# PEER block: u rows gathered for 64 more tokens, and all dense u ahead of all dense v

## Chip, cores and metric

The kernel runs on one core of a Trainium2 chip. The metric is the device time of one execution in microseconds (us). Engines are named as in the profile: PE is TensorE (PEld its weight loads), DVE VectorE, ACT ScalarE, POOL GpSimd, SP the queue that issues most transfers.

## What is computed

One decoder layer over 512 tokens of width 2048: a mixer (attention and mLSTM heads, not touched here), its output projection, and PEER, a layer with 16384 single-neuron experts. Each token takes 16 experts for each of 8 heads; cut to what matters:

```python
q = (xt @ w_q).reshape(T, PEER_HEADS, 2, PEER_KEY_DIM // 2)
scores = jnp.einsum('thpd,pnd->thpn', q, keys)
s_top, i_top = lax.top_k(scores, PEER_TOPK)
cand = ...            # 16 x 16 sums of the two halves
s_fin, pos = lax.top_k(cand, PEER_TOPK)
gate = jax.nn.softmax(s_fin, axis=-1)
ub = jnp.take(u, ib, axis=0)
act = jax.nn.gelu(jnp.einsum('thkd,td->thk', ub, xb), approximate=False) * gb
vb = jnp.take(v, ib, axis=0)
y = jnp.einsum('thk,thkd->td', act, vb)
```

## The kernel before, in words

The 512 tokens are four token tiles of 128. Token tile 0 is done sparsely: for each of its 128 (head, choice) slots POOL gathers one row of u for each token (128 rows of 8 KB in one indirect transfer, L588), DVE forms the dot with the normalised activations (L603); later the same with v (L614). The other three tiles, ND = 384 tokens, are done densely: TensorE multiplies all 128 blocks of 128 experts (u products into `sacc`, 48 matmuls a block, 384 columns each), and the chosen experts' gates stand in a table over all experts, zero elsewhere. The table is made with one-hot vectors: for each token two one-hots of 128 columns (`o`, one of them weighted with the gates, L887 and L893) are multiplied on TensorE (`gp_`), copied into `stg` by ACT (L896) and stored to memory (`gtab`). u products times gates, split into two parts, are `wbuf`; v products (`y`, 512 columns each) have them as weights. A group is 8 blocks; NEARLY = 68 blocks' u products are made early, beside the expert choice and the gate tables (`early_steps`, stored in `stab`), the other 60 between the v products of the groups that need them (`gated`, L938).

Every matrix is multiplied in two parts: `stream_split` (L101) loads 512 KB into one of three `raw` buffers, ACT casts the upper part `hi` (L109), DVE subtracts the lower part `lo` (L111), and TensorE takes hi and lo in three products. A new `raw` can be loaded when both have read the old one.

The order on each engine is made by a scheduler at build time from the order of the program and its priorities; a lower part gets its place 35 instructions earlier. Each engine then runs strictly in that order. The gathers are paced: `advance(n)` issues n of them at a place in the program, and each waits for the ACT cast before it (L590). Three `row` buffers hold the rows, two of them ahead of the one in use. SP issues all other transfers in one order, and one that waits holds up those behind it.

Stages in the profiled execution: mixer up to 636 us; output projection, with token tile 0's queries and choice, to about 921; choice for tiles 1 to 3 to 1374; gate tables to 1660; then u and v to the end.

Of the kernel before, what the change touches and what calls it, by code (L numbers as in the profile page):

```python
# [81 lines left out]
def block_kernel(ctx: ExitStack, tc: tile.TileContext, a, out):  # L82
# [35 lines left out]
    def project_nat(psA, src, parts, hook=None):  # L118
        """[tokens, 512 columns] of part.T @ w, one bank for each token tile."""
# [16 lines left out]
    def project_t(psA, src, xT):  # L136
        """[256 columns, tokens] of w.T @ xT, one bank for each 128 columns."""
# [27 lines left out]
    def transpose_split(psB, src, dst, groups=range(4)):  # L165
        """src [128 tokens, 2048] -> dst [128, hi/lo, kc, tokens]."""
# [28 lines left out]
    with ExitStack() as mx:  # L195
# [43 lines left out]
        # gates in rows: 0..7 fox forget, 32..35 mlstm input, 64..67 mlstm forget  # L239
# [5 lines left out]
        def gate_rows():  # L245
            # x2 is free until the mixer's first heads: 16 slots of 512 columns
# [24 lines left out]
            # log1p(ex) = ln(u) + (ex - (u - 1)) / u  # L271
# [11 lines left out]
            # fox: F = cumsum(log_sigmoid), in two parts in rows 0.. and 32.. of cF, with ones in  # L283
            # rows 64.. and 96..; bF has ones against the parts and -F against the ones
# [11 lines left out]
            # mlstm: b = within-chunk cumsum, e = i - b  # L296
# [13 lines left out]
            # running maximum M of e (from the state's), m = b + M  # L310
# [25 lines left out]
        def gate_cols(rowx, ones4, mprev, Mr):  # L336
            # columns: 0.. exp(-m), 32.. exp(m_prev - M), 64.. exp(e - M_last), 96.. exp(m_prev - M_last)
# [175 lines left out]
        def head_norms(t, lo, n, width):  # L513
            """heads of `width` columns from column lo, in place."""
# [24 lines left out]
        # from here on the transposed mixer output, then the transposed x3  # L539
        xtx.close()  # L540
        xdp = ctx.enter_context(tc.tile_pool(name="xdp", bufs=1, side="right"))
# [14 lines left out]
    stab = gdram.tile([NEARLY, P, ND], F32, name="stab")  # L556
    gtab = gdram.tile([NTG, P, NI * TG], F32, name="gtab")

    def tpool(stack, name, bufs=1):
        return stack.enter_context(tc.tile_pool(name=name, bufs=bufs, reuse_waits="tile"))  # L560
# [3 lines left out]
    idx0 = pc.tile([P, SLOTS], I32, name="idx0")  # L564
    gate0 = pc.tile([P, SLOTS], F32, name="gate0")
    dots = pc.tile([P, SLOTS], F32, name="dots")
    act0 = pc.tile([P, SLOTS], F32, name="act0")
    rows = tpool(ctx, "rows", 3)

    def dense_steps(ps, tag, i0, dst):  # L570
        """dst = gelu(u x3) of expert block i0, [experts, dense tokens], in 8 steps."""
        acc = ps.tile([P, 512], F32, tag=tag, name="sacc")[:, 0:ND]
        for s in range(2):
            hi, lo = stream_split(a["uT"][i0, s])
# [8 lines left out]
        nc.scalar.activation(out=dst, in_=acc, func=AF.Gelu)  # L583
        yield

    def gather(src, j):
        row = rows.tile([P, D], F32, tag="row", name="row")
        ins = nc.gpsimd.indirect_dma_start(  # L588
            out=row, out_offset=None, in_=a[src],
# [4 lines left out]
        return row  # L594

    def sparse_steps():
        ahead = []
        for j in range(SLOTS + LAG):
            if j < SLOTS:
                ahead.append(gather("u", j))  # L600
# [53 lines left out]
    with ExitStack() as rx:  # L654
# [190 lines left out]
        for _ in first:  # L845
            pass
# [220 lines left out]
```

## Time and profile before

| | us |
|---|---|
| median of 3 runs | 3297.2 (3293.05 to 3298.24) |
| profiled execution, its own time | 3298.24 |
| its span, first to last instruction | 3298.2 |
| PE busy | 3245.6 (98%) |
| DVE busy | 2293.9 (70%) |
| ACT busy | 1242.8 (38%) |
| POOL busy | 473.8 (14%) |

The durations of matmuls in the profile overlap, as they are pipelined; the time that one costs is the distance from its start to the next one's. The chain of work that ended last is followed back from the last instruction, at each step to what released it. A group's "idle before" is the idle time of its engine just ahead of its instructions. The granted clock was 0.996 of full speed over the span.

### The profile page before, as it was taken

The numbers are of one execution on the slowest core, as the hardware profiler recorded it, in microseconds if no ns is written. First come the engines' busy times: TensorE is split into PE (matmuls) and PEld (weight loads), VectorE is DVE, ScalarE is ACT, GpSimd is POOL, SyncE is SP. The second block draws the span as 40 slices with busy tenths as digits, with TensorE's granted clock in tenths as the row PEclk, the third lists the DMA queues.
The fourth block names the chain that finished last, engine by engine and source line by source line (L and its number), as shares of the span: only waits on it lengthen the run. The fifth ranks groups of instructions, "written<-read, shape, count | busy, mean of one in ns | idle before, by whom it ended". The sixth has DMA issues, their size and how long they took to land.

```text
span 3298.2 us, 43394 instructions
## 1 busy us (share of the span) xinstructions
PE 3245.6 (98%) x16681; PEld 2886.8 (88%) x16681; DVE 2293.9 (70%) x3746; ACT 1242.8 (38%) x1667; POOL 473.8 (14%) x380
## 2 busy tenths in 40 slices
PE   8999999999999999999999999999999999999998
PEld 6788787778799999999998888888899899898997
DVE  5542324467888989988867778876777767677774
ACT  4432223355554444455533333333233233232333
POOL 0000000100112323200012211111211112122110
PEclk9999999999999999999999999999999999999999
DMA  4232232266657667676788888887787887777774
GB/s 149 77 90 83 77 96 71 84 228 198 218 166 250 232 244 259 231 252 223 252 319 301 309 302 300 314 307 273 277 287 272 295 283 272 281 279 273 283 269 140
DMA packets 194065, 751.69 MB, mean 228 GB/s; under 512 B 19265, under 2 KB 61505, under 8 KB 158145
## 3 DMA queue, kind: packets, MB, share of 16 engines
q1 hardware_dynamic: 156994, 480.47, 41.8%
q0 software_dynamic: 36864, 268.45, 22.8%
q8 instruction: 131, 2.15, 0.3%
q14 instruction: 76, 0.62, 0.1%
HBM read 706.12 MB, written 42.73 MB: 227 GB/s over the span
## 4 chain that ended last, share of the span: by engine, by line
PE 73%; DMA 8%; issue 8%; DVE 7%; POOL 2%; ACT 1%; POOLq 0%; DVEq 0%; SPq 0%; ACTq 0%
PE y L116 24%; PE acc L116 22%; PE sacc L116 21%; DMA row<-in_u,idx 3%; DMA row<-in_v,idx 2%; DVE lo L111 2%; POOL row L588 2%; DMA raw<-in_w_out 1%; DVE x L614 1%; DMA stab<-es 1%; DMA raw<-in_uT 1%; PE sps L116 1%; ACT hi L109 1%; PE po L116 1%; DVE row L603 1%
## 5 line engine op out<-in xcount | busy, mean ns | idle before, releaser
L109 ACT CAST hi<-raw 128x1024 fp32r<-128x1024 f32 x736 | 773.8, 1052 | 1525.7 <-PE y L116 505.3
L111 DVE TENSOR_TENSOR lo<-raw,hi 128x1024 fp32r<-128x1024 f32 x736 | 900.6, 1227 | 514.4 <-ACT hi L109 513.3
L116 PE MATMUL sacc<-x3d,hi 128*128 128x384 f32 x4096 | 1052.7, 337 | 0.4 <-ACT x3d L173 0.4
L116 PE MATMUL y<-hi,wbuf 128*128 128x512 f32 x3048 | 942.0, 390 | 0.0
L116 PEld LDWEIGHTS sacc<-x3d,hi 128*128 128x128 f32 x4096 | 735.1, 188 | 1.2 <-ACT x3d L173 0.6
L116 PE MATMUL sacc<-x3d,lo 128*128 128x384 f32 x2048 | 686.0, 335 | 1.9 <-DVE lo L111 1.9
L116 PEld LDWEIGHTS y<-hi,wbuf 128*128 128x128 f32 x3048 | 572.9, 188 | 118.8
L116 PE MATMUL y<-lo,wbuf 128*128 128x512 f32 x1524 | 594.4, 390 | 5.2 <-DVE lo L111 5.0
L614 DVE SCALAR_TENSOR_TENSOR x<-row,act,x 128x2048 f32<-128x2048 f32 x128 | 300.9, 2351 | 138.3 <-DMA row<-in_v,idx 137.2
L116 PEld LDWEIGHTS sacc<-x3d,lo 128*128 128x128 f32 x2048 | 385.0, 188 | 4.4 <-DVE lo L111 4.4
L603 DVE SCALAR_TENSOR_TENSOR row<-row,x 128x2048 f32<-128x2048 f32 x128 | 293.8, 2295 | 120.3 <-DMA row<-in_u,idx 120.2
L116 PEld LDWEIGHTS y<-lo,wbuf 128*128 128x128 f32 x1524 | 286.4, 188 | 67.1 <-DVE lo L111 7.9
L588 POOL DMA_INDIRECT row<-in_u,idx x128 | 196.4, 1534 | 822.7 <-ACT hi L109 377.8
L588 POOL DMA_INDIRECT row<-in_v,idx x128 | 182.4, 1425 | 778.3 <-ACT hi L109 673.5
L116 PE MATMUL acc<-xT,hi 128*128 128x512 f32 x768 | 243.8, 395 | 0.0
L116 PE MATMUL acc<-hi,xT 128*128 128x512 f32 x768 | 241.8, 393 | 0.0
L116 PEld LDWEIGHTS acc<-hi,xT 128*128 128x128 f32 x768 | 143.8, 188 | 28.5
L116 PEld LDWEIGHTS acc<-xT,hi 128*128 128x128 f32 x768 | 143.7, 189 | 28.4 <-ACT xT L173 0.3
L116 PE MATMUL acc<-lo,xT 128*128 128x512 f32 x384 | 151.1, 393 | 0.0
L116 PE MATMUL acc<-xT,lo 128*128 128x512 f32 x384 | 150.4, 392 | 0.0
L156 POOL TENSOR_TENSOR rsr<-rst,mhalf 128x1 f32<-128x1 f32 (+2 forms) x24 | 19.0, 795 | 838.5 <-DVE rst L153 735.6
L893 DVE TENSOR_SCALAR o<-cst,i0T,gT 128x128 f32<-128x128 f32 x384 | 113.8, 345 | 35.5 <-PE gp__12799 L116 1.3
(522 smaller groups left out, 3073.6 us busy)
## 6 DMA issues: line engine op xcount, KB each, us to landing
raw<-in_uT SPq DMA_DIRECT2D x256, 512.0 KB, 5.0
raw<-in_vS SPq DMA_DIRECT2D x256, 512.0 KB, 5.1
raw<-in_w_out SPq DMA_DIRECT2D x64, 512.0 KB, 4.3
raw<-in_w_q SPq DMA_DIRECT2D x64, 512.0 KB, 4.5
gtab<-stg SPq DMA_DIRECT2D x12, 2048.0 KB, 7.5
gt<-gtab SPq DMA_DIRECT2D x16, 1536.0 KB, 9.8
raw<-in_w_fqk SPq DMA_DIRECT2D x32, 512.0 KB, 3.6
stab<-es SPq DMA_DIRECT2D x68, 192.0 KB, 4.4
```

What stands on the lines that cost most here:

```text
L109: pace[0] = nc.scalar.copy(out=hi[:, :width], in_=raw[:, :width]).ins
L111: nc.vector.tensor_tensor(out=lo[:, :width], in0=raw[:, :width], in1=hi[:, :width].bitcast(F32), op=OP.subtract)
L116: nc.tensor.matmul(out=o, lhsT=l, rhs=r, start=start, stop=stop)
L156: nc.gpsimd.tensor_tensor(out=r, in0=t, in1=mhalf[:, 0:width], op=OP.pow)
L588: ins = nc.gpsimd.indirect_dma_start(out=row, out_offset=None, in_=a[src], in_offset=bass.IndirectOffsetOnAxis(ap=idx0[:, j:j + 1], axis=0))
L603: nc.vector.scalar_tensor_tensor(out=row, in0=row, scalar=1.0, in1=x30, op0=OP.mult, op1=OP.mult, accum_out=dots[:, j - LAG:j - LAG + 1])
L614: nc.vector.scalar_tensor_tensor(out=x2[:, 0, :], in0=row, scalar=act0[:, j - LAG:j - LAG + 1], in1=x2[:, 0, :], op0=OP.mult, op1=OP.add)
L893: nc.vector.tensor_scalar(out=o0, in0=iota, scalar1=i0T[:, t:t + 1], scalar2=gT[:, t:t + 1], op0=OP.is_equal, op1=OP.mult)
```

## The change

1. Of token tile 1, the first NS = 64 tokens leave the dense u products, whose matmuls have DU = 320 columns in place of 384. Their u rows are gathered: 64 tokens x 128 slots are laid over 128 partitions as two halves of 64 slots, so 64 more gathers and dots. Their activations come back through a transpose (`act1`) into the gate table as weights, so v stays dense for all 384 tokens.
2. All 128 blocks of u products now come ahead of all v products. 118 of them are made beside the choice (2 + 56), ten gate tables (30) and alone (30); HOLD = 10 are kept for the last two tables, those of the 64 tokens, which need the gathered dots. Their results are stored to memory and read back two blocks at a time.
3. In the v stage the weights `wbuf` have two buffers, so that one group's are made beside the products of the group before; the first 512 columns' accumulators (`yk`) stay in PSUM over all groups. y has five banks in place of six.
4. In the gate tables one DVE comparison of 1024 columns makes the one-hots of both keys of four tokens (`on`), and ACT weights one of them (`og`).
5. The first four heads' queries of token tile 0 come ahead of the output projection of tiles 2 and 3; the gathers start there. The softmax of the gates is done once for each token tile.

```diff
-NEARLY = 68
-EARLY_TOPK = (1, 1, 2)
-EARLY_0 = 3
-EARLY_G = 2
-PACE_EARLY = 1.4
-PACE_G = 1.0
-PACE_V = 1.0
+NS = 64
+R = P // NS
+S1 = SLOTS // R
+DU = ND - NS
+FIRST_HEADS = 4
+EARLY_0 = 2
+EARLY_TOPK = (2, 2, 3)
+EARLY_G = 3
+HOLD = 10
+PACE_O = 0.4
+PACE_EARLY = 1.15
+PACE_G = 1.5
+PACE_U = 1.5
...
-                mm(acc, uh, x3d[:, 0, kc, :], kc == 0, False)
-                mm(acc, uh, x3d[:, 1, kc, :], False, False)
-                mm(acc, ul, x3d[:, 0, kc, :], False, kc == KC - 1)
+                mm(acc, uh, x3d[:, 0, kc, NS:], kc == 0, False)
+                mm(acc, uh, x3d[:, 1, kc, NS:], False, False)
+                mm(acc, ul, x3d[:, 0, kc, NS:], False, kc == KC - 1)
...
+        for r in range(R):
+            nc.sync.dma_start(out=x30[r * NS:(r + 1) * NS], in_=x1d)
+        while not ready1[0]:
             yield
+        yield from gathered("u", lambda j: idx1[:, j:j + 1], S1, dot(dots[1]), lambda j: True)
+        nc.scalar.activation(out=dots[1], in_=dots[1], func=AF.Gelu)
+        nc.vector.memset(act1, 0.0)
+        for r in range(R):
+            rs = slice(r * NS, (r + 1) * NS)
+            nc.vector.tensor_tensor(out=act1[rs, r * S1:(r + 1) * S1], in0=dots[1][rs],
+                                    in1=gate1[rs], op=OP.mult)
+        u_over[0] = True
...
+        for _ in range(4 * FIRST_HEADS):
+            next(scores0, None)
+            next(chosen, None)
+        transpose_split(psB, x31, parts[1])
         for n in range(4):
             out_proj(n, (2, 3), hook)
+            for _ in range(2):
+                next(scores0, None)
...
+                on = n3.tile([P, 2, 4, P], F32, tag="on", name="on")
+                nc.vector.tensor_tensor(
+                    out=on, in0=iota[:, None, None, :].to_broadcast([P, 2, 4, P]),
+                    in1=idxT[:, :, t4:t4 + 4, None].to_broadcast([P, 2, 4, P]), op=OP.is_equal)
+                for q in range(4):
+                    og = n3.tile([P, P], F32, tag="og", name="og", bufs=6)
+                    nc.scalar.activation(out=og, in_=on[:, 0, q, :], func=AF.Copy,
+                                         scale=gT[:, t4 + q:t4 + q + 1])
+                    mm(gp_[:, q, :], on[:, 1, q, :], og, True, True)
...
+        for tg in range(NS // TG, NTG):
+            table(tg, EARLY_G)
+            advance(PACE_G * EARLY_G)
+        while nearly[0] < NI - HOLD:
+            early_s()
+            advance(PACE_U if not u_over[0] else 0.0)
+        while not u_over[0]:
+            advance(1.0)
+        pt = psB.tile([P, ND], F32, tag="ps", name="pt")
+        nc.tensor.transpose(pt[:, 0:P], act1, ident)
+        for r in range(R):
+            rs = slice(r * S1, (r + 1) * S1)
+            nc.scalar.copy(out=gT[rs, 0:NS], in_=pt[rs, r * NS:(r + 1) * NS])
+        for tg in range(NS // TG):
+            table(tg, EARLY_G)
...
+    load_gates(0)
+    while nearly[0] < NI - 2:
+        early_s()
...
+            acc = kept if n == 0 else [psY.tile([P, 512], F32, tag="y", name="y", bufs=5)
+                                       for _ in range(NT - 1)]
...
+                if s == 1 and not last:
+                    gated((g + 1) * NSV + n)
```

Three places show what the scheduler made of it. On PE, in the output projection of tiles 2 and 3 (`x3d`, 512 columns): a step of token tile 0's queries (`x30T`, 256 columns, 12 products) stood between two steps of the projection before.

```order
L116 MATMUL acc_5519<-hi_5744,x3d_4755 128x512 x2
L116 MATMUL acc_5519<-lo_5745,x3d_4755 128x512
L116 MATMUL acc_5519<-hi_5744,x3d_4755 128x512
L116 MATMUL acc0_5723<-hi_5762,x30T_4759 128x256
L116 MATMUL acc0_5723<-lo_5763,x30T_4759 128x256
```

In the change, 16 such steps stand together, one after the other: the weights change from one buffer (`hi_5622`) to the next (`hi_5640`) with nothing between.

```order
L122 MATMUL acc0_5583<-lo_5623,x30T_4759 128x256
L122 MATMUL acc0_5583<-hi_5622,x30T_4759 128x256
L122 MATMUL acc0_5583<-hi_5640,x30T_4759 128x256
L122 MATMUL acc0_5583<-lo_5641,x30T_4759 128x256
L122 MATMUL acc0_5583<-hi_5640,x30T_4759 128x256 x2
```

Each step still needs its own 512 KB of weights. On DVE, at the end of the gathers: `row,dots` is a dot over a gathered row, `lo` a lower part of u's weights, `act` the activations of the 64 tokens, `on` the one-hots of the last two tables.

```order
L640 SCALAR_TENSOR_TENSOR row,dots_4842<-row,x_4830 128x2048
L117 TENSOR_TENSOR lo<-raw,hi 128x1024
L640 SCALAR_TENSOR_TENSOR row,dots_4842<-row,x_4830 128x2048
L117 TENSOR_TENSOR lo<-raw,hi 128x1024
L640 SCALAR_TENSOR_TENSOR row,dots_4842<-row,x_4830 128x2048
L117 TENSOR_TENSOR lo<-raw,hi 128x1024
L661 TENSOR_TENSOR act_4843<-dots_4842,gate_4840 64x64 x2
L117 TENSOR_TENSOR lo<-raw,hi 128x1024
L940 TENSOR_TENSOR on<-cst,idxT 128x1024 x2
L117 TENSOR_TENSOR lo<-raw,hi 128x1024
L940 TENSOR_TENSOR on<-cst,idxT 128x1024 x6
```

The dots alternate with lower parts, and 14 of the 16 comparisons of the last two tables stand behind the last dot, with the multiplication that follows it. On SP, where u ends and v begins: `gtab<-stg` stores a table, `gtA<-gtab` loads the first group's gates from all of them, `stab<-es` stores a block of u products.

```order
L109 DMA raw<-in_vS 128x1024
L609 DMA stab<-es 128x320
L109 DMA raw<-in_vS 128x1024 x2
L952 DMA gtab<-stg 128x4096
L609 DMA stab<-es 128x320
L109 DMA raw<-in_vS 128x1024
L978 DMA gtA<-gtab 128x12x256
L987 DMA sv<-stab 128x2x320 x3
```

Before, the loads of u's weights for further blocks stood around the same load:

```order
L901 DMA gtab<-stg 128x4096
L103 DMA raw<-in_uT 128x1024 x2
L643 DMA stab<-es 128x384
L103 DMA raw<-in_uT 128x1024
L934 DMA gt<-gtab 128x12x256
L103 DMA raw<-in_uT 128x1024
L643 DMA stab<-es 128x384
```

The load of the gates now stands behind the store of the last block of u, and only v's weights and the stored u follow it.

## Rows read from the trace of the kernel before

**Rows 1.** The page, part 1: busy us, share of the span, instructions.

```profile
PE 3245.6 (98%) x16681; PEld 2886.8 (88%) x16681; DVE 2293.9 (70%) x3746; ACT 1242.8 (38%) x1667; POOL 473.8 (14%) x380
```

**Rows 2.** The page, part 4: shares of the chain that ended last.

```profile
PE 73%; DMA 8%; issue 8%; DVE 7%; POOL 2%; ACT 1%; POOLq 0%; DVEq 0%; SPq 0%; ACTq 0%
```

**Rows 3.** Windows: choice, tables, v alone; columns in the first line.

```profile
core 0: us, PE busy (x) PEld busy (x) DVE busy (x) ACT busy (x) POOL busy (x), PEclk, DMA share, GB/s
921.00:1374.00 453.00, 442.63 (x2558) 437.08 (x2557) 402.87 (x1162) 202.13 (x277) 128.28 (x125) 1.00 0.67 235
1374.00:1660.00 286.00, 286.00 (x1915) 286.00 (x1915) 246.11 (x554) 163.98 (x169) 12.70 (x13) 0.99 0.66 234
1790.00:2260.00 470.00, 468.73 (x2068) 387.72 (x2067) 370.27 (x433) 149.03 (x176) 92.38 (x56) 1.00 0.84 304
```

**Rows 4.** The chain in order of time: start, us, what; end stretch.

```profile
2295.10 65.32 PE y L116 x288
...
2360.42 66.58 PE sacc L116 x384
```

**Rows 5.** Timeline of PE: start, us, what; queries of token tile 0.

```profile
807.19 0.28 PE L116 MATMUL acc<-lo,x30T 128*128 128x256 f32 x1
807.31 0.40 PE L116 MATMUL acc<-hi,x30T 128*128 128x256 f32 x2
807.55 0.28 PE L116 MATMUL acc<-lo,x30T 128*128 128x256 f32 x1
```

**Rows 6.** The page, part 5: busy, mean ns | idle before, releaser.

```profile
L109 ACT CAST hi<-raw 128x1024 fp32r<-128x1024 f32 x736 | 773.8, 1052 | 1525.7 <-PE y L116 505.3
L111 DVE TENSOR_TENSOR lo<-raw,hi 128x1024 fp32r<-128x1024 f32 x736 | 900.6, 1227 | 514.4 <-ACT hi L109 513.3
...
L116 PEld LDWEIGHTS sacc<-x3d,hi 128*128 128x128 f32 x4096 | 735.1, 188 | 1.2 <-ACT x3d L173 0.6
...
L603 DVE SCALAR_TENSOR_TENSOR row<-row,x 128x2048 f32<-128x2048 f32 x128 | 293.8, 2295 | 120.3 <-DMA row<-in_u,idx 120.2
```

**Rows 7.** Groups with shapes apart, whole span; columns as in rows 6.

```profile
L887 DVE TENSOR_TENSOR o<-cst,i1T 128x512 f32<-128x512 f32 x96 | 65.9, 686 | 1.2 <-PE gp__12058 L116 0.4
...
L583 ACT ACTIVATE es<-sacc 128x384 f32<-128x384 f32 x68 | 33.1, 486 | 2.5 <-DMA stab<-es 2.1
...
L518 ACT ACTIVATE sq<-x 128x128 f32<-128x128 f32 x32 | 9.9, 309 | 14.9 <-DVE x L496 14.3
...
L444 ACT ACTIVATE x<-num,rd 128x256 f32<-128x256 f32 x16 | 8.1, 507 | 2.6 <-DVE rd L443 2.3
...
L518 ACT ACTIVATE sq<-x 128x256 f32<-128x256 f32 x16 | 6.7, 416 | 1.2 <-DVE rst L153 0.7 <-DVE x L537 0.3
```

**Rows 8.** Timeline: two evacuations of a table's four-token steps.

```profile
1401.88 1.12 ACT L896 COPY stg<-gp__12319 128x512 f32<-128x512 f32 x1 [1.58 <-PE gp__12319 L116]
...
1404.85 1.12 ACT L896 COPY stg<-gp__12347 128x512 f32<-128x512 f32 x1
```

**Rows 9.** Windows of 5 and 20 us; columns as in rows 3.

```profile
1745.00:1750.00 5.00, 4.92 (x22) 3.73 (x22) 3.44 (x3) 1.06 (x2) 0.00 (x0) 1.00 1.03 430
2140.00:2160.00 20.00, 20.00 (x90) 16.57 (x89) 13.13 (x14) 4.92 (x6) 1.88 (x2) 1.00 0.97 371
```

**Rows 10.** Waits from 636 to 960: in total, times, longest.

```profile
PEld acc L116 <- DVE lo L111: 11.6, 13, 2.3
...
PE acc L116 <- DVE lo L111: 7.7, 10, 1.9
```

**Rows 11.** The page, parts 3 and 6: the gathers' queue; issues to landing.

```profile
q0 software_dynamic: 36864, 268.45, 22.8%
...
raw<-in_w_q SPq DMA_DIRECT2D x64, 512.0 KB, 4.5
gtab<-stg SPq DMA_DIRECT2D x12, 2048.0 KB, 7.5
gt<-gtab SPq DMA_DIRECT2D x16, 1536.0 KB, 9.8
```

More of the change, by code (lines that the diff above doesn't have):

```diff
@@ L582, in dense_steps @@
                     yield
-        nc.scalar.activation(out=dst, in_=acc, func=AF.Gelu)
+        sv = esp.tile([P, DU], F32, tag="es", name="es")
+        nc.scalar.activation(out=sv, in_=acc, func=AF.Gelu)
+        nc.sync.dma_start(out=stab[b], in_=sv)
         yield
[L586 to L589, printed above, removed]
-            in_offset=bass.IndirectOffsetOnAxis(ap=idx0[:, j:j + 1], axis=0))
-        tc.add_manual_dep(ins.ins, pace[0].name,
-                          mybir.DependencyInfo(mybir.DependencyClass.Sync,
-                                               mybir.DependencyReason.DATA), reason="pace")
-        return row
@@ L596, in sparse_steps, with early_s @@
[L596 to L617 removed]
+    def early_s():
+        for _ in early_steps():
+            pass
@@ new lines, in block_kernel, with gathered @@
+    late = {}
+    heads0, ready1, u_over = [0], [False], [False]
+    def gathered(src, idx, n, use, ready):
+        ahead = []
+        for j in range(n + LAG):
+            while j < n and not ready(j):
+                yield
+            if j < n:
+                row = rows.tile([P, D], F32, tag="row", name="row")
+                ins = nc.gpsimd.indirect_dma_start(
+                    out=row, out_offset=None, in_=a[src],
+                    in_offset=bass.IndirectOffsetOnAxis(ap=idx(j), axis=0))
+                tc.add_manual_dep(ins.ins, pace[0].name,
+                                  mybir.DependencyInfo(mybir.DependencyClass.Sync,
+                                                       mybir.DependencyReason.DATA), reason="pace")
+                ahead.append(row)
+            if j >= LAG:
+                use(ahead.pop(0), j - LAG)
+            yield
@@ L792, in x3_row @@
             return rows.tile([P, D], F32, tag="row", name="x3")
-        def first_steps():
-            norm2(0, x30)
-            yield
-            x31 = norm2(1, x3_row())
-            yield
-            for t, x3 in ((0, x30), (1, x31)):
-                for g in (0, 2):
-                    transpose_split(psB, x3, parts[t], range(g, g + 2))
-                    yield
-            yield from w_q0()
         def choose0_steps():
@@ L809, in choose0_steps @@
                 yield from choose(0, h, sc0[:, h])
-        ready = [0]
-        first = first_steps()
+            gates(0)
+        scores0 = w_q0()
         chosen = choose0_steps()
-        def hook():
-            next(first, None)
-            next(chosen, None)
         def load_x(t):
@@ new lines, in block_kernel, with load_gates @@
+        nc.tensor.transpose(pt[:, 0:P], act1, ident)
+        for r in range(R):
+            rs = slice(r * S1, (r + 1) * S1)
+            nc.scalar.copy(out=gT[rs, 0:NS], in_=pt[rs, r * NS:(r + 1) * NS])
+        for tg in range(NS // TG):
+            table(tg, EARLY_G)
+    va = tpool(ctx, "va", 2)
+    wbufs = [va.tile([P, 2, GB, ND], F32R, name="wbufA", bufs=1), None]
+    gtb = [va.tile([P, NTG, GB, TG], F32, name="gtA", bufs=1), None]
+    def load_gates(g):
+        gt = gtb[g % 2]
+        nc.sync.dma_start(out=gt.rearrange("p g i q -> p g (i q)"),
+                          in_=gtab[:, :, g * GB * TG:(g + 1) * GB * TG].rearrange("g p x -> p g x"))
@@ L905, in block_kernel @@
+    load_gates(0)
+    while nearly[0] < NI - 2:
+        early_s()
+    load_s(0)
+    load_s(1)
+    for k in range(2):
+        gated(k)
+    while nearly[0] < NI:
+        early_s()
+    for k in range(2, GB // 2):
+        gated(k)
+    xds.close()
     ph.close()
-    psY = ctx.enter_context(tc.tile_pool(name="psY", bufs=6, space=PSUM, reuse_waits="tile"))
-    psS = ctx.enter_context(tc.tile_pool(name="psS", bufs=2, space=PSUM, reuse_waits="tile"))
+    vb = tpool(ctx, "vb", 2, side="right")
@@ L965, in block_kernel @@
         for n in range(3 if last else 4):
-            if n == 2 and not last:
-                gt = load_gates(g + 1)
             if n == 2 and last:
@@ L973, in block_kernel @@
                     parts.append((s, stream_split(a["vS"][g, 3, s], to=row)))
[L974 to L975 removed]
+            acc = kept if n == 0 else [psY.tile([P, 512], F32, tag="y", name="y", bufs=5)
+                                       for _ in range(NT - 1)]
+            for s in range(NSV):
                 hi, lo = stream_split(a["vS"][g, n, s])
                 for j in range(NT - 1):
[L978 to L983 removed]
+                    v_products(acc[j], g, hi, lo, s, j, s == 0 and (n > 0 or g == 0),
+                               s == NSV - 1 and (n > 0 or last))
+                if not last:
+                    advance(RATE)
+                if s == 1 and not last:
+                    gated((g + 1) * NSV + n)
+                    if n == 3 and g + 2 < NG:
+                        load_gates(g + 2)
@@ L984, in block_kernel @@
             for j in range(NT - 1):
-                if not last:
+                if last:
+                    add_block(dn.tile([P, 512], F32, tag="wf", name="sq5"), acc[j], 1 + j, n)
+                elif n > 0:
                     xs = x2[:, 1 + j, n * 512:(n + 1) * 512]
                     nc.vector.tensor_tensor(out=xs, in0=acc[j], in1=xs, op=OP.add)
-                else:
-                    add_block(dn.tile([P, 512], F32, tag="wf", name="sq5"), acc[j], 1 + j, n)
-    parts += [(s, stream_split(a["vS"][NI // GB - 1, 3, s])) for s in range(2, GB // 2)]
+    parts += [(s, stream_split(a["vS"][NG - 1, 3, s])) for s in range(2, NSV)]
```

284 lines of the change are left out of this document (142 added, 142 removed).

## The prediction

> **What bounds the kernel now.** Read the engine table and the chain's shares first: TensorE is busy for 98% of the span, VectorE for 70% [rows 1], and 73% of the chain that ended last is TensorE itself [rows 2]. So time leaves this kernel only where TensorE's own work leaves it, and comes back wherever TensorE is made to wait. The windows by stage then show where there is no room left: in the expert choice VectorE is at 89% and TensorE still loses 10.4 us of 453; in the gate tables TensorE loses nothing; in the stretch of v alone it loses 1.3 us of 470 at 304 GB/s [rows 3].
>
> What one matmul costs is its spacing, since the durations overlap. In the chain in order of time, 288 v products of 512 columns take 65.32 us, 226.8 ns each, and 384 u products of 384 columns take 66.58 us, 173.4 ns each [rows 4]. In the timeline three matmuls of 256 columns start 0.36 us apart, 120 ns each [rows 5]. The three lie on a line, 0.417 ns a column and 13 ns on top; 320 columns come to **146.7 ns**.
>
> **The change, part by part** (times in us, summed against the profiled execution: 3298.2, which is 1.0 above the median of 3297.2).
>
> *Removed.* (A) 128 blocks x 48 u products go from 384 to 320 columns: 6144 x 26.7 ns = **-163.9**. The rest of TensorE's work is kept; y stays at 512 columns. 45 additions of y, the per-head softmaxes and 384 weightings of one-hots leave VectorE, worth nothing by themselves: it was not the bound there.
>
> *Added or moved.*
> (B) 16 of the 32 steps of token tile 0's queries now run with no projection between them. A step is 12 x 120 ns = 1.44 of TensorE, but its weights come through three buffers: landing 4.5 [rows 11], cast 1.05, lower part 1.23 [rows 6], 6.8 / 3 = 2.3. 13 steps (three are prefetched) lose 0.86 each, 11 [rows 5, 6, 11]; the other steps, now in twos and fours, an estimated 3 more. Before, TensorE waited 19.3 there for lower parts, weight loads included [rows 10]. **+14**, from 0 if the scheduler's order hides it to 30 if the choice queues ahead of lower parts.
> (C) A head of the choice is now 96 x 173.4 ns + 7 x 48 x 146.7 ns = 65.9 of TensorE. VectorE before: 89% [rows 3] of about 51 a head is 45.5, less 5.6 dots of 2.30 and 12 lower parts of 1.23 [rows 6], leaves 6.0 for each token tile's choice. Now 9.2 x 2.30 + 18 x 1.23 + 3 x 6.0 = 61.3, 93% (a little less without the softmax). At the 2.3% that the stage lost, 538 in place of about 410 lose 3 more; **+4**, from 0 to 25.
> (D) Ten tables run beside three u blocks each. TensorE: 144 x 146.7 ns + 8 x 0.89 = 28.2 (a four-token step starts every 2.97 [rows 8], less 12 x 173.4 ns, is 0.89). VectorE: 8 comparisons of 1024 columns at about 1.22 (the rate of a lower part, and of the 512-column row [rows 7]), 6 lower parts, 4.5 dots: 27.5. ScalarE: 32 weightings, 8 evacuations of 1.12 [rows 8], 6 casts, 3 gelus of 0.49 [rows 7]. A 128-column activation with a constant scale takes 0.31; one of 256 columns with a scale per partition takes 0.51 against 0.42 with a constant [rows 7], so I take 0.40, and ScalarE needs 29.6. If neighbours overlap so that a weighting costs 0.31, ScalarE needs 26.7 and this term is near 0. Three engines within 6% of each other, each in order: I take 29.6 and the 2.3% that the choice stage loses, 30.3. **+21**, from 0 to 45.
> (E) 30 u blocks run with 1.5 gathers each: 1.049 MB of weights, 0.164 stored, 1.57 gathered (268.45 MB over 256 gathers [rows 11]), 2.79 MB in 7.04, 396 GB/s. Five microseconds at 430 GB/s exist, but over twenty the best row is 371 [rows 9]: from 0 to 30 x 0.48 = 14. **+8**. The Trainium skill (HBM Reference, Specifications) gives about 358 GB/s as a core's share of its memory and about 425 for a core that streams alone; by the first, E would be an estimated +22, by the second 0, and the 430 row [rows 9] speaks for the second.
> (F) The last 17 gathers are issued with no pace between them, beside held-back blocks; VectorE's order alternates dot and lower part. A pair moves 1.66 MB per 3.52 of TensorE: 0.33 to 0.94 over by the same two rates. **+10**, from 0 to 35 if the three row buffers set the pace.
> (G) The last two tables need those gathers, and only 130 u products (19.1) and 16 x 0.89 = 14.2 of TensorE stand behind act1's transpose. ScalarE needs 64 x 0.40 + 16 x 1.12 + 5 casts + 2 gelus = 49.8 against 33.3. **+16**, from 8 to 20.
> (H) Behind the last table only 14 u products (2.1) are left. The last evacuation 1.1, the table's store 7.5, its load 9.8 [rows 11], product and cast 1.6: 20.0 less 2.1, **+18**, from 12 to 26. On SP the load stands behind the last block's store of u, which waits for its gelu; five v loads stand ahead of it, so the queue adds no more. Before, u blocks covered the same pair of transfers.
> The v stage moves 20.8 MB a group in 65.3, 319 GB/s, close to the 304 at which TensorE lost 0.3% [rows 3]: 0, to 10. y has five banks in place of six, which costs nothing while VectorE takes an accumulator out within the 2.7 of the next 12 products. The copies of x3, indices and gates through memory cost nothing under the 30 u blocks of E, 211 of TensorE; bare, they would be three or four landings of about 5.
>
> Sum: 14 + 4 + 21 + 8 + 10 + 16 + 18 = 91; 3298.2 - 163.9 + 91 = **3225**.
>
> **The rivals.**
> *Covers hold.* The scheduler's order absorbs B to F, ScalarE overlaps its activations; G 8, H 14 and a few remain: 3298.2 - 163.9 + 25 = 3160. For it: the tables stage of before, all busy, lost nothing [rows 3]. Against: VectorE was at 86% there, now at 98%.
> *The transfers bind.* At the 371 of [rows 9], or lower, E and F take their upper ends and C and D lose with them: about 3225 + 6 + 6 + 13 to 38 = 3250 to 3275. For it: no twenty microseconds went above 371. Against: share 1.03 at 430.
> *Slower: VectorE stops at rows that have not landed.* From the first u block to the first y, VectorE has 288 lower parts (353), 179 dots (412; 13 of the 192 come earlier), 96 comparisons (117) and 24 choices (144), 1026; TensorE 901 of u, 133 of queries (768 x 173.4 ns) and 85 of tables (96 x 0.89), 1119. Before, VectorE idled 120.3 in front of 128 u dots, 0.94 each [rows 6]. Lower parts are queued behind, so TensorE waits too. My 43 for C to F is 0.76 a row; from 1.17 the kernel is slower than before (179 x 1.17 + 1026 = 1235, and 1235 - 1119 with the 48 of B, G and H is 164); at 1.5 it takes 3298.2 - 163.9 + 48 + 175 = 3357. For it: 64 more rows, closer together, on three buffers. Against: part of the 0.94 was slack of an engine that ran ahead.
> *It does not do what it says.* Weight loads are busy 286.0 of 286.0 in the tables stage [rows 3], 188 ns each [rows 6]. If they bind, 320 columns take 173.4 as well: 3298.2 + 91 = 3389. Against: the 256-column rows load weights of the same size every 120 ns [rows 5], so the load's duration is no spacing. The Trainium skill (Perfetto Trace Analysis, Identifying the Most-Contended Engine) judges TensorE's room by this busy share of weight loads; by that rule A would be 0 and the time an estimated 3389, which the 120 ns contradict.
>
> **How the numbers follow.** Forecast, 3205 to 3240, 0.44; covers hold 0.24; transfers bind 0.15; VectorE stops 0.10; weight loads bind 0.03; within 0.2% (6.6, about what a measurement here tells from no change) 0.04. Faster 0.83, same 0.04, slower 0.13. The range takes in the first three: 3155 to 3290 leaves out about 0.17.
>
> **What would show it.** After: 320-column u products 147 ns apart; the u stage at VectorE above 90% and DMA near 1; idle TensorE of about 18 between the last u product and the first y, released by the gate table's load; some 25 at act1's transpose and the two tables behind it, released by ScalarE. A spacing of 173 ns, or idle time in front of dots near 1.2 a row with TensorE waiting for lower parts, would make the prediction wrong; so would a transition that is covered.

## The result, and the profile after

The changed kernel takes 3348.8 us (median of 4 runs, 3342.74 to 3359.63) against 3297.7 for the kernel before on the same chip (4 runs, 3293.05 to 3300.69): ratio **1.0161, with an interval of 1.0141 to 1.0181**. It is slower by 51 us, where 73 less were forecast. The profiled execution took 3342.7, with a span of 3341.0.

The page's engine table and its chain by engine and by line, after (before: [rows 1, 2]):

```profile
PE 3149.4 (94%) x16682; PEld 2758.9 (83%) x16682; DVE 2323.1 (70%) x3251; ACT 1281.3 (38%) x1957; POOL 642.2 (19%) x444
...
PE 39%; issue 24%; DMA 18%; DVE 11%; POOL 4%; ACT 3%; POOLq 0%; DVEq 0%; SPq 0%; ACTq 0%
PE acc L122 20%; PE y L122 10%; DMA row<-in_u,idx 9%; DVE lo L117 4%; POOL row L627 3%; DMA row<-in_v,idx 3%; PE sacc L122 3%; DMA raw<-in_uT 3%; PE yk L122 2%; DMA raw<-in_vS 2%; DVE row L640 1%; ACT hi L115 1%; DMA raw<-in_w_out 1%; PE sps L122 1%; DMA raw<-in_w_q 1%
```

TensorE was 98% busy and made 73% of the chain; now it is 94% busy and makes 39%. VectorE's share is 70% as before, and says nothing. The chain's place was taken by "DMA row" (12%) and "issue" (24%, before 8%; most of it lies ahead of gathers that wait to be issued).

The removal itself came out as worked. The timeline of PE after, in the expert choice (start, us, what):

```profile
1422.05 0.31 PE L122 MATMUL sacc<-x3d,lo 128*128 128x320 f32 x1
1422.20 0.46 PE L122 MATMUL sacc<-x3d,hi 128*128 128x320 f32 x2
1422.49 0.31 PE L122 MATMUL sacc<-x3d,lo 128*128 128x320 f32 x1
1422.64 0.46 PE L122 MATMUL sacc<-x3d,hi 128*128 128x320 f32 x2
1422.93 0.31 PE L122 MATMUL sacc<-x3d,lo 128*128 128x320 f32 x1
```

Three products of 320 columns start 0.44 us apart, 146.7 ns each: term A is -163.9. So the profiled span of 3341.0 holds 3341.0 - 3298.2 + 163.9 = 207 us of new loss. Where it lies is read from windows whose bounds are the first dense u product (945), the first gate table (1555), the last u product (2219) and the first v product (2237):

```profile
core 0: us, PE busy (x) PEld busy (x) DVE busy (x) ACT busy (x) POOL busy (x), PEclk, DMA share, GB/s
945.00:1555.00 610.00, 577.82 (x3713) 567.07 (x3712) 529.27 (x1225) 206.07 (x272) 201.54 (x157) 0.99 0.77 278
1555.00:2219.00 664.00, 606.64 (x4089) 591.22 (x4087) 505.52 (x445) 374.67 (x689) 158.66 (x105) 0.97 0.87 331
2219.00:2237.00 18.00, 0.00 (x0) 0.00 (x0) 5.97 (x5) 1.46 (x4) 1.58 (x1) 0.55 1.02 362
2237.00:3341.00 1104.00, 1064.09 (x4608) 873.40 (x4608) 790.28 (x675) 339.70 (x404) 232.16 (x130) 0.98 0.79 282
```

The work in each is its matmuls times their spacing (u 146.7 ns, 173.4 before; v 226.8; a table's four-token step 0.89); the u products of the choice are counted in the window's groups:

| stretch | before | after | work changes by | new loss | forecast |
|---|---|---|---|---|---|
| projection, queries (up to the first u product) | 917 | 945 | 0 | **28** | B 14 |
| expert choice | 464 | 610 | 2822 u products for 1710: +117.5 | **28** | C 4 |
| tables and u blocks | | 664 | work 572.7 | **91** | D to G 55 |
| up to the first v product | | 18 | | **18** | H 18 |
| v stage | | 1104 | work 1045.1 | **41** | 0 |

Behind the choice the kernel before took 1917 us for work of 1899, so 17.7 of loss are taken off the v stage's 59, which holds the same end. The five make 206.

What ended the idle time, after (engine, line, waited for: us, times, longest; whole span):

```profile
ACT hi L115 <- DMA raw<-in_uT: 323.1, 106, 8.6
...
DVE x L668 <- DMA row<-in_v,idx: 202.2, 84, 8.6
ACT hi L115 <- DMA raw<-in_vS: 182.0, 47, 12.4
DVE row L640 <- DMA row<-in_u,idx: 160.9, 92, 6.5
...
ACT og L945 <- DVE on L940: 51.4, 31, 4.6
...
PE sacc L122 <- DVE lo L117: 47.4, 36, 6.1
...
PE acc L122 <- DVE lo L117: 23.1, 25, 4.3
...
PE yk L122 <- ACT wbufA L1001: 19.2, 1, 19.2
...
PE y L122 <- DVE lo L117: 18.0, 12, 4.9
...
PE y L122 <- DVE x L1080: 6.5, 1, 6.5
```

TensorE's stops behind 945 us come to 139 us: 78 for lower parts, 24 for weighted one-hots in the tables (ScalarE waits there for VectorE's comparisons), 19 before the first v product. Ahead of the lower parts two things are late: rows (VectorE stands 160.9 before u rows, 0.84 each, and 202.2 before v rows, 1.58 each; before 120.3, 0.94 each, in u [rows 6], and 137.2, 1.07 each, in v by part 5 of its page) and the weights (ScalarE stands 505 before u and v weights). Waits of an engine with room cost nothing by themselves, so the traces leave two theories for the longest part. **V**: VectorE stands at a row, and the lower parts queued behind it reach TensorE late. **M**: gathers, weights and stores share the memory, and the weights themselves land too late for three raw buffers.

One such stop, at a group's end in the v stage: SP's issues, then GpSimd's gather, VectorE, and TensorE (start, us, what, idle before and its releaser):

```profile
2521.31 1.71 SPq L987 DMA_DIRECT2D sv<-stab  x2
2523.07 0.47 SPq L978 DMA_DIRECT2D gtB<-gtab  x1
2523.78 8.07 SPq L109 DMA_DIRECT2D raw<-in_vS  x3
```

```profile
2524.77 6.41 POOL L627 DMA_INDIRECT row<-in_v,idx  x1 [8.97 <-ACT hi L115]
```

```profile
2530.28 1.22 DVE L117 TENSOR_TENSOR lo<-raw,hi 128x1024 fp32r<-128x1024 f32 x1
2539.61 2.35 DVE L668 SCALAR_TENSOR_TENSOR x<-row,dots,x 128x2048 f32<-128x2048 f32 x1 [8.11 <-DMA row<-in_v,idx]
2541.88 2.35 DVE L117 TENSOR_TENSOR lo<-raw,hi 128x1024 fp32r<-128x1024 f32 x2
```

```profile
2543.15 0.79 PE L122 MATMUL y<-lo,wbufA 128*128 128x512 f32 x1 [4.95 <-DVE lo L117]
```

Two loads of stored products, the 1.57 MB of gates and a gather are issued within 4 us. The row lands 14.8 us after its issue, VectorE stands 8.11, two lower parts come behind it at once, and TensorE has stood 4.95 for the first of them. This is V and M in one, and experiments must part them.

### The profile page after: what moved, and what is told of

The parts are those of the page before. It is cut to its first block, busy times and chain, and to the rows that moved or that the text cites. A ratio compares the mean times of both kernels' runs of the same rounds, so it can differ in the third digit from the quotient of the medians.

```text
span 3341.0 us, 43311 instructions
## 1 busy us (share of the span) xinstructions
PE 3149.4 (94%) x16682; PEld 2758.9 (83%) x16682; DVE 2323.1 (70%) x3251; ACT 1281.3 (38%) x1957; POOL 642.2 (19%) x444
## 4 chain that ended last, share of the span: by engine, by line
PE 39%; issue 24%; DMA 18%; DVE 11%; POOL 4%; ACT 3%; POOLq 0%; DVEq 0%; SPq 0%; ACTq 0%
PE acc L122 20%; PE y L122 10%; DMA row<-in_u,idx 9%; DVE lo L117 4%; POOL row L627 3%; DMA row<-in_v,idx 3%; PE sacc L122 3%; DMA raw<-in_uT 3%; PE yk L122 2%; DMA raw<-in_vS 2%; DVE row L640 1%; ACT hi L115 1%; DMA raw<-in_w_out 1%; PE sps L122 1%; DMA raw<-in_w_q 1%
## 5 line engine op out<-in xcount | busy, mean ns | idle before, releaser
L122 PE MATMUL sacc<-x3d,hi 128*128 128x320 f32 x4096 | 929.8, 315 | 0.0
L122 PE MATMUL sacc<-x3d,lo 128*128 128x320 f32 x2048 | 648.1, 316 | 47.8 <-DVE lo L117 47.4
L640 DVE SCALAR_TENSOR_TENSOR row<-row,x 128x2048 f32<-128x2048 f32 x192 | 441.6, 2302 | 164.7 <-DMA row<-in_u,idx 160.9
L668 DVE SCALAR_TENSOR_TENSOR x<-row,dots,x 128x2048 f32<-128x2048 f32 x128 | 300.9, 2351 | 205.5 <-DMA row<-in_v,idx 202.2
L122 PE MATMUL y<-hi,wbufA 128*128 128x512 f32 x1152 | 361.0, 394 | 6.7 <-DVE x L1080 6.5
L122 PE MATMUL y<-hi,wbufB 128*128 128x512 f32 x1128 | 354.0, 394 | 4.1 <-ACT hi L115 4.1
L122 PEld LDWEIGHTS y<-hi,wbufA 128*128 128x128 f32 x1152 | 219.1, 190 | 53.5 <-DVE x L1080 6.9
L122 PEld LDWEIGHTS y<-hi,wbufB 128*128 128x128 f32 x1128 | 214.5, 190 | 49.8 <-ACT hi L115 5.0
L122 PE MATMUL y<-lo,wbufA 128*128 128x512 f32 x576 | 227.0, 394 | 11.6 <-DVE lo L117 11.6
L122 PE MATMUL y<-lo,wbufB 128*128 128x512 f32 x564 | 222.3, 394 | 6.4 <-DVE lo L117 6.4
```

The lines of the kernel that those rows point to most:

```text
L122: nc.tensor.matmul(out=o, lhsT=l, rhs=r, start=start, stop=stop)
L640: nc.vector.scalar_tensor_tensor(out=row, in0=row, scalar=1.0, in1=x30, op0=OP.mult, op1=OP.mult, accum_out=to[:, j:j + 1])
L668: nc.vector.scalar_tensor_tensor(out=x2[:, 0, :], in0=row, scalar=dots[0][:, j:j + 1], in1=x2[:, 0, :], op0=OP.mult, op1=OP.add)
```

## Experiments

The changed kernel is "after"; lengths of stretches are from one profiled execution each, times are medians.

**1. Rows gathered but not read.**

```diff
-  scalar_tensor_tensor(out=row, in0=row, scalar=1.0, in1=x30, ...)
+  scalar_tensor_tensor(out=x30, in0=x30, scalar=0.0, in1=x30, ...)
-  scalar_tensor_tensor(out=x2[:, 0, :], in0=row, ...)
+  scalar_tensor_tensor(out=x2[:, 0, :], in0=x30, ...)
```

> The changed kernel with its rows still gathered, but no VectorE instruction reads them: the 192 dots and the 128 additions of v keep their size and place and work on x30 in place of the row, so VectorE never waits for a gather and every transfer remains (the results of the gathered tokens are left out). Theory V, VectorE stands at rows that have not landed and the lower parts of the weights queue behind it: the 161 us and 202 us of VectorE idle before rows go, TensorE's idle from 600 us on falls from 154 to about 70, with it most of the about 100 us at the lower clock, and the time falls by 70 to 120 to 3225 to 3275. Theory M, the weights themselves land late because gathers, weights and stores share the memory: the time stays within 15 of the changed kernel's 3343 and ScalarE still waits for raw weights as before.

**2. No gathers either.** As 1, and `gathered` issues none. Both leave out the results of the gathered rows.

> As the run above, but the 320 gathers are left out as well (335.56 MB), so neither a row nor its traffic is there; VectorE's work is kept. Theory V: no better than the run above by more than 15, about 3215 to 3260. Theory M: here and only here the loss goes, 3215 to 3250, and 50 or more below the run above. Above 3300 neither holds, and the loss lies in the order of the stages themselves. Left in any case: about 19 us before the first v product and some at the last two tables.

Measured: 3260.5 (0.9889 of before, 0.9856 to 0.9921) and 3180.6 (0.9645, 0.9617 to 0.9672). Windows with the same bounds, of run 1 and of run 2 (columns as above):

```profile
944.00:1553.00 609.00, 580.00 (x3716) 569.92 (x3717) 599.61 (x1290) 207.62 (x275) 214.89 (x157) 0.98 0.77 278
1553.00:2184.00 631.00, 593.88 (x4093) 585.29 (x4093) 571.04 (x443) 373.43 (x695) 193.15 (x105) 0.97 0.92 356
2184.00:3256.00 1072.00, 1050.89 (x4609) 864.43 (x4607) 648.75 (x608) 338.93 (x401) 226.34 (x131) 1.00 0.80 293
```

```profile
931.00:1540.00 609.00, 579.09 (x3713) 568.74 (x3712) 602.62 (x1291) 206.86 (x275) 92.69 (x81) 0.98 0.45 148
1540.00:2123.00 583.00, 578.18 (x4098) 576.97 (x4097) 573.07 (x443) 375.50 (x696) 0.00 (x0) 0.99 0.57 198
2123.00:3177.00 1054.00, 1045.10 (x4611) 864.75 (x4609) 644.17 (x605) 339.23 (x401) 2.21 (x4) 1.00 0.50 170
```

Both theories hold, half and half: VectorE's waiting is worth 88 (with it goes a gather's waiting for a row buffer), the gathers' traffic another 80. Not all of the 168 is new loss, since the kernel before issues 256 of the 320 gathers too. The weights land sooner without the traffic; us from issue to landing, the median, in run 1 and in run 2 (before 5.0):

```profile
raw<-in_uT SPq DMA_DIRECT2D x256, 512.0 KB, 5.8
```

```profile
raw<-in_uT SPq DMA_DIRECT2D x256, 512.0 KB, 3.3
```

Tables and u blocks go from 664 to 631 to 583 (work 573), the v stage from 1104 to 1072 to 1054 (work 1045). TensorE's stops for weighted one-hots, 24 us in after, are 0.2 in run 2. The 18 us before the first v product go in run 1 already, where the last dot of u starts at 1900 in place of 2172. One stretch does not move: the choice stays at 609 with VectorE at 603 of 609.

**3. Four raw weight buffers.**

```diff
-  raw = stream.tile([P, 1024], F32, tag="raw", name="raw", bufs=3)
+  raw = stream.tile([P, 1024], F32, tag="raw", name="raw", bufs=4)
```

> The changed kernel with four buffers for raw weights in place of three. Theory M: 20 to 60 us faster than the changed kernel (ScalarE's 323 us of waiting for raw u weights halves, since a landing of 8 us is then covered by four products' time of 3.5 each). Theory V: within 8 of it, since the weights wait behind VectorE and not for their transfer.

Room for it comes from two small tiles that keep one buffer less. Measured: 3306.0 (1.0031, 1.0014 to 1.0048), 43 less than after. Its waits:

```profile
ACT hi L115 <- DMA raw<-in_uT: 59.7, 21, 10.7
...
ACT hi L115 <- DMA raw<-in_vS: 40.1, 13, 9.2
```

ScalarE's 323.1 and 182.0 fall to 59.7 and 40.1. The gain lies ahead of the v stage: queries 12, choice 15, tables and u blocks 25 (639). The v stage takes 1106 in place of 1104: late weights cost nothing there that this profile shows, in the u stage they do. M holds for the u stage.

**4. Gathers evenly spaced** (inside the tables, and at half blocks).

> The changed kernel with the gathers issued evenly: inside a gate table eight times 0.56 in place of 4.5 at its end, and beside each half of a held-back u block. Theory V with bunched rows as its cause: 20 to 50 us faster, most of it between 1560 and 2210 us. Theory M: 10 to 30 faster there, because weights and rows no longer collide in bursts. If bunching is not the cause: within 8.

Measured: 3382.2 (1.0262, 1.0224 to 1.0300), 33 *slower*: a miss. Dots now stand between a table's comparisons, and ScalarE waits for comparisons 86.8 in place of 51.4; tables and u blocks take 689 in place of 664. The bunch behind the table was the better place. But the v stage, whose instructions stand in the same order as in after on VectorE, GpSimd and SP, took 1126 here and 1104 there: the same order came out 22 apart, so smaller differences between single profiles of this stage show nothing.

**5. Four row buffers; 6. the same in the v stage with four raw buffers.**

> The changed kernel with four row buffers and three rows ahead in place of three and two, from token tile 0's last queries on and through the v stage (room from one buffer less of weighted one-hots and the final norm written in place). Theory R, VectorE stands at a row because it is asked for too late: the idle time before v rows falls from 202 to under 100 us and before u rows from 161 to under 110, the v stage (1104 us from the first v product to the end) falls to about 1080, tables and u blocks (664 us) to about 640: 3290 to 3315 in all. Theory M, rows are late because the transfers are full: asking earlier only moves the queue, within 12 of 3349.

> Four raw weight buffers, and four row buffers in the v stage alone. Theory R: as the run with four raw buffers (3306) up to the first v product, and a v stage of about 1080 in place of its 1107: 3275 to 3292. Theory M: 3298 to 3312, the v stage as before.

Measured: 3338.5 (1.0140, 1.0102 to 1.0178) and 3306.6 (1.0022, 0.9998 to 1.0047). VectorE's idle time before v rows stays at 206.9 and 213.5, the v stage at 1119 and 1107. One more row on its way buys nothing there. In run 5 tables and u blocks fall to 647, near the 640 of theory R, but its v stage and the gap ahead of it (24 in place of 19) are longer; theory R falls for the v stage. VectorE has room in this stage and runs up to the next row that has not landed, however early that was asked for, so the sum of these waits is no measure of the loss.

**7. Queries between the projection's steps,** with four raw buffers.

> Four raw weight buffers, and one step of token tile 0's queries beside each step of the projection in place of 16 in one burst and the rest behind. If the burst is what loses time there (28 us against before from 600 us to the first dense u product, 345 against 317): the first dense u product comes 12 to 20 us earlier than with four raw buffers alone (933), and the time is 3286 to 3296. If the loss lies in the choice of token tile 0 on VectorE, which now comes later: no gain there, 3303 to 3325.

Measured: 3317.4 (1.0070, 1.0043 to 1.0097), 11 slower than run 3; the first u product comes at 946 in place of 933, and the gap before the first v product grows from 18 to 38. Spreading the queries this way gains nothing; since the choice of token tile 0 comes later with them, the run does not part the two.

**8. Without the 64 rows of token tile 1.**

```diff
-  yield from gathered("u", lambda j: idx1[:, j:j + 1], S1, dot(dots[1]), lambda j: True)
+  nc.vector.memset(dots[1], 0.0)
```

> The changed kernel without the 64 gathers of token tile 1 and their 64 dot products; dense u stays at 320 columns (the results of 64 tokens are left out). It prices that part. If the added rows are what fills VectorE and the transfers between tables and the last u block: tables and u blocks fall from 664 to 595 to 620 us and the 18 before the first v product go, 3265 to 3290. If they cost what the forecast gave them (20 to 30 in all): 3318 to 3330.

The results of the 64 tokens are left out. Measured: 3285.9 (0.9958, 0.9939 to 0.9976). The 64 rows cost 63, nearly 1 us each, and their 163.9 of matmuls is what they buy. Tables and u blocks take 613, and the 18 are gone; the v stage is no shorter (1116). So most of the new loss is not these rows': without them the kernel still loses some 152 of the 163.9 (3285.9 against 3297.7). That part comes with the rest of the change: the new order of stages, and the same weights and token tile 0's rows in 164 us less of TensorE's work. No run parts these, as one with the new order and 384 columns would.

**9. Gates in quarters; 10. and with four raw buffers.**

```diff
-  if n == 3 and g + 2 < NG:
-      load_gates(g + 2)
+  if g + 2 < NG:
+      load_gates(g + 2, slice(3 * n, 3 * n + 3))
```

> The changed kernel with a group's gates (1.57 MB in pieces of 1 KB) loaded in four quarters over the group before, in place of one load per group right behind two loads of stored u products and in front of the weights. Theory G, the v stage loses its time where that load, a gather and the weights collide once a group (a gather that landed in 14.8 us, VectorE 8.1 us idle before its row, TensorE stopped): the v stage falls from 1104 to 1065 to 1085, the time by 20 to 40 to 3310 to 3330. Theory M, the transfers of the stage are too many wherever they stand (319 GB/s needed): within 10 of 3349.

> The same with four raw weight buffers. If the two losses are separate places they add: 3306 less what the quarters alone bring, 3265 to 3290 by theory G, 3295 to 3312 by theory M.

(`load_gates` now takes the tables to load.) Measured: 3336.3 (1.0131, 1.0096 to 1.0167) and 3287.9 (0.9965, 0.9951 to 0.9979). Beside four raw buffers the quarters bring 18 (from 3306.0), and the intervals do not meet; beside three they bring 12, and the intervals overlap. The v stage takes 1091 and 1092 (1103 in run 12), against 1104 to 1126 in the eight profiled executions with the load in one piece that read their v rows (after, 3 to 8, 13 below), and 1100 in a ninth (15). Theory G expected 1065 to 1085. So the load in one piece costs something, less than theory G had it, and where the 18 lie single profiles do not tell. The second of these versions beats the kernel before.

**11. The kernel before with half the descriptor space.** The change also halves the space in which the gathers' descriptors stand (`dynamic_dma_scratch_size=8192`), so this is a rival for the late rows.

> The kernel before with the descriptor space of the gathers halved to 8192 bytes, which the change did too. If the halved space holds gathers back: before slows by 10 or more, and GpSimd's gather instructions in the v stage grow from 1425 ns towards the 1808 of the changed kernel. If not: within 0.3% and 1425 ns as before.

Measured: 3298.4 (1.0002, 0.9990 to 1.0015). GpSimd's gather instructions in v grow from 1425 ns to 1586, and the time stays:

```profile
L588 POOL DMA_INDIRECT row<-in_v,idx x128 | 203.1, 1586 | 753.5 <-ACT hi L109 658.7 <-DVE x L614 67.5 <-issue 10.2
```

**12. Fourteen u blocks held back,** with four raw buffers and quarters.

> Four raw buffers, gates in quarters, and 14 u blocks held back behind the gathers in place of 10, so that four more stand beside and behind the last two tables. If the 18 us before the first v product are only a lack of cover: 8 to 18 below the run without it. If the four blocks are missed just as much as cover for the gathers: within 6.

Measured: 3292.1 (0.9969, 0.9946 to 0.9991), 4 from run 10. The gap shrinks from 18 to 14 only.

**13. No u rows at all:** neither gathers nor dots of u; the results of the gathered tokens are left out.

> The changed kernel without any u row: no gathers and no dot products of u (the results of the gathered tokens are left out), v rows as they are. Taking the gathers alone away left the expert choice as long as it was, 609 us against 611 from the first dense u product to the first gate table, with VectorE at 599 of 605. Theory D, VectorE's own work fills that stretch, dots ahead of their time in that run: without the dots it falls to 560 to 580 and the first dense u product comes 10 to 25 us earlier (945); the tables and u blocks take about 580 in place of 664, 3185 to 3215 in all. If the choice is held up by its own steps or by the weights: it stays above 600, 3220 to 3245.

Measured: 3200.8 (0.9697, 0.9663 to 0.9731). Windows:

```profile
930.00:1498.00 568.00, 561.57 (x3691) 558.93 (x3690) 363.92 (x1073) 202.31 (x269) 52.03 (x81) 1.00 0.47 158
1498.00:2079.00 581.00, 576.60 (x4102) 575.92 (x4101) 287.89 (x241) 384.08 (x694) 1.98 (x1) 0.99 0.56 195
```

The choice falls from 610 to 568 once VectorE has 364 us of work there in place of 529: theory D holds. (Run 2 kept 609 without the gathers: VectorE, no longer waiting, made 33 more dots in this stretch, 109 in place of 76.) The first u product comes 15 us earlier (930), as in run 2 (931).

**14. Lower parts earlier** in VectorE's order, with four raw buffers and quarters; **15. that alone; 16. 140 places.**

```diff
-AHEAD_LO = 35
+AHEAD_LO = 70
```

> Four raw buffers and gates in quarters, and the lower parts of the weights 70 places earlier in VectorE's order in place of 35. Theory V, lower parts stand behind rows that have not landed: they pass more rows now, TensorE's idle time before lower parts (47 in u and 18 in v in the changed kernel) halves, 3262 to 3280 against 3288 without it. If the place in the queue does not matter, because a lower part is there as soon as its weights are: within 8. If the rows that are passed keep their buffers longer and gathers come late: 8 or more slower.

> The changed kernel with nothing but the lower parts 70 places earlier in VectorE's order in place of 35. Theory V: the v stage falls from 1104 to 1070 to 1085 (26 went in it with raw buffers and quarters as well), tables and u blocks stay, 3310 to 3330. If it worked only together with the quarters or the fourth raw buffer: within 10 of 3349.

> Four raw buffers, quarters, and the lower parts 140 places earlier. If more rows are still passed: 5 to 15 below the 3270 of 70 places, now among tables and u blocks. If 70 already passes every row that a weight buffer reaches: within 6. If VectorE now stands at lower parts whose weights have not landed, with rows and choices behind: slower by 8 or more.

Measured: 3270.5 (0.9921, 0.9896 to 0.9946), 3339.0 (1.0128, 1.0102 to 1.0153), 3279.8 (0.9944, 0.9925 to 0.9964). Run 14's v stage:

```profile
2187.00:3253.00 1066.00, 1051.62 (x4608) 867.57 (x4608) 790.11 (x675) 340.54 (x405) 215.80 (x130) 0.99 0.80 292
```

Run 14 is the fastest version with all its work, 0.8% below the kernel before and 78 us below the change. But 140 places are no better than 70 (v stage 1086), and 70 alone bring 10, with intervals that overlap: not the 19 to 39 that theory V expected, but what was expected if it works only together with the others (v stage 1100). So 70 places bring 17 beside four raw buffers and quarters; whether by the mechanism of V or by another order around it stays open.

## Why the prediction was wrong

**A, the spacing of 146.7 ns, was right,** and so was the rejection of the weight loads as a bound. Its steps B to H summed to 91 where 207 went; each is taken with what it measured.

- **The v stage (0, up to 10): 41,** and 22 more in run 4's profile, with the same order there. **This is the largest miss, and the step that failed is "319 GB/s, close to the 304 at which TensorE lost 0.3% [rows 3]".** The mean rate was carried over, but not what was packed together: two stored-product loads, a gate load and a gather within 4 us at a group's end, and VectorE in front of the row with lower parts behind. Of the stage's 1104, 32 go without reading rows (run 1) and 18 more without their traffic (run 2), which leaves 1054 for work of 1045. The 18 are within the 22 by which this stage varies, the 32 and the 50 are not. Splitting the gate load brings 18 beside four raw buffers (run 10).
- **C, the choice (+4, up to 25): 28.** The failed step is "93%", taken as room with the 2.3% lost before. VectorE's work was sized within 8% (490 for the eight heads), but an in-order engine's load is its work and its waits together: 529 us busy, and

```profile
DVE row L640 <- DMA row<-in_u,idx: 48.7, 38, 4.6
...
DVE lo L117 <- ACT hi L115: 27.6, 19, 3.5
```

  between 945 and 1555, 605 of 610. There was no room. Run 13 takes 165 us of VectorE work away, and 42 us of time go; a fourth raw buffer alone takes 15 (run 3), so late weights have a part in it.
- **D to G (55): 91.** The ten tables, the u blocks alone and the last two tables, after:

```profile
1554.00:1868.00 314.00, 292.65 (x2045) 287.72 (x2044) 249.69 (x220) 240.96 (x486) 68.16 (x44) 0.97 0.85 319
1868.00:2176.00 308.00, 275.56 (x1796) 269.30 (x1796) 231.65 (x206) 93.70 (x117) 89.01 (x60) 0.97 0.94 364
2176.00:2218.00 42.00, 39.44 (x259) 35.20 (x257) 24.18 (x21) 40.01 (x90) 1.49 (x1) 0.96 0.51 182
```

  The work in them is 277, 263 and 33. D (+21) measured 37, and its step, ScalarE's 29.6 a table, failed: with the same tables and no gathers 1 is lost there (run 2). What ScalarE waits for are VectorE's comparisons, which stand behind rows and dots. E and F together (+18) measured 45. They priced the transfers by bytes and rate, and gave a late weight or row no price of its own; without the 64 rows the u blocks lose 0.3 (run 8). G (+16) measured 9, with ScalarE busy for 40 of 42 as foreseen. In the whole stretch weights that land late with three buffers cost 25 (run 3), VectorE's waits 33 (run 1), the gathers' traffic 48 more (run 2, part of it the same as run 3's).
- **H (+18): 18,** released by the load of the gates as foreseen (19.2 in the waits). But it hangs on F: where the u rows end early (runs 1, 2, 8, 13) the last tables stand among u blocks and the gap is gone.
- **B (+14, up to 30): 28.** The size was within its bounds; the working, a burst that three buffers feed too slowly, is not shown: spreading the queries gains nothing (run 7), a fourth raw buffer gives back 12, and leaving out the u gathers 14 to 15 (runs 2, 13). The 19.3 that TensorE is said to have waited before counts the same stops twice, at the weight load and at the product behind it [rows 10]; it is 11.6, and not in the sum.

**The clock had no term.** The granted clock over the span was 0.979 (before 0.996): 3341.0 x 0.021 = 70 us of full clock not granted, against 13. Some of it fell on an idle TensorE. Windows around the first v product:

```profile
2210.00:2220.00 10.00, 7.46 (x52) 6.67 (x51) 6.10 (x5) 8.33 (x15) 2.42 (x2) 1.00 0.68 249
2220.00:2230.00 10.00, 0.00 (x0) 0.00 (x0) 1.79 (x2) 0.00 (x0) 0.65 (x1) 0.53 0.98 360
2230.00:2240.00 10.00, 2.96 (x7) 2.08 (x8) 5.75 (x6) 3.08 (x7) 0.00 (x0) 0.50 1.08 352
2240.00:2250.00 10.00, 10.00 (x43) 8.22 (x42) 7.71 (x9) 5.62 (x9) 1.17 (x1) 0.94 0.87 271
```

TensorE stands still here, the granted clock goes to the lower of its two levels (0.50, 1.2 GHz), and it is back while the next products run. Summed over windows of 10 us, (1 - clock) x busy time is 45 us after and 7 before: up to 38 of the 207 are products that ran at the lower level, as those right behind this stop did (in the timeline three v products take 1.41 us from 2237.6 and 0.68 from 2242.1).

**The rivals.** "VectorE stops at rows that have not landed" named the sign and, with 3357, nearly the time, but it was given 0.10 and its gauge misled: it asked for 1.17 us of idle time a row, and 0.84 were measured, less than before. The sum of waits does not tell, since much of it is slack. Runs 1 and 2 show why the gauge failed: half of the rows' cost is their traffic, and a third of what VectorE's waiting cost lay in the v stage, which the rival left out. "The transfers bind" had the other half, at 25 to 50 where some 80 were lost. Chances of 0.15 and 0.10 were set against each other where both came true. The Trainium skill (HBM Reference, Specifications) gives about 358 GB/s as a core's share of its memory and about 425 for a core that streams alone; after's windows of 10 us reach 419 GB/s (2120 to 2130, DMA share 1.02), so the second agrees, as the forecast held; but in that window TensorE was busy for 7.62 of the 10.

## What to carry to other kernels

Price a row that is gathered by three things, not by its bytes: what VectorE does with it, what is queued behind its wait, and how much later everything else lands. Here 64 rows cost 63 us. Shorter matmuls do not shorten what runs beside them: without those rows 152 of the 164 us that TensorE saves were still lost. For an in-order engine add its waits to its work in the stage at hand before calling the rest room, and count buffers by the landing time under the new load, not by the one of before: a fourth weight buffer (4 KB a partition) gave back 43 us. Of the versions with all their work only those with four raw buffers and gates in quarters beat the kernel before; with lower parts earlier as well it is 3270, 0.992 of it.

## What was not expected of the hardware

A gather's instruction on GpSimd is long where VectorE is busy. In the v stage of after, 41 of 126 took about 0.94 us, with VectorE busy for 43% of that time; the other 85 took 2.23 on average, with VectorE busy for 95% of it. In the stop shown above the instruction took 6.41 and ended when VectorE's run of instructions did (2531.2 and 2531.5); VectorE then stood 8.11 us for that very row. The Trainium skill (SBUF — State Buffer, "SBUF: two separate sides") says that GpSimd cannot write the descriptors of its transfers while VectorE runs an operation in a two-port mode, which locks the port that the two share. The trace agrees in direction; which of VectorE's operations here lock it no run shows, the profile's spans on GpSimd are rough, half the descriptor space lengthens the instruction too (run 11), and no run separates any of this from the transfer's own delay.
